# S5 rotation in place, outputs from four products, GLU's first blocks four tiles at a time beside the last S5 blocks

## The chip, the cores and the metric

The kernel runs on one core of one Trainium2 chip. The metric is the device time of one launch in microseconds (us). The kernel before takes 2421.26 us, the median of three runs that lie between 2420.5 and 2422.59 us.

## What is computed

One inference step of a two-layer decoder with 2048 channels, for 256 prompt positions and 8 sample rows (264 columns in all), in float32. Layer 0 is a retention and HGRN2 mixer, layer 1 an S5 state-space layer followed by a GELU-GLU, and each layer ends in a SwiGLU FFN. The change lies in layer 1's mixer, the middle of the program:

```python
def _s5(u, h0_re, h0_im, lam_re, lam_im, log_dt, b_re, b_im, c_re, c_im, d_skip):
    ...
    _, _, hr, hi = lax.associative_scan(_complex_affine_combine, (a_r, a_i, bu_r, bu_i), axis=1)
    y = (jnp.einsum('gcp,blgp->blgc', c_re.astype(jnp.float32), hr)
         - jnp.einsum('gcp,blgp->blgc', c_im.astype(jnp.float32), hi)
         + d_skip.astype(jnp.float32).reshape(S5_GROUPS, S5_GROUP) * ug)
    return y.reshape(B, L, D_MODEL), hr[:, -1], hi[:, -1]

def _odd_mixer(h, s_re, s_im, lam_re, lam_im, log_dt, b_re, b_im, c_re, c_im, d_skip, w_a, w_b):
    y, hr, hi = _s5(h, s_re, s_im, lam_re, lam_im, log_dt, b_re, b_im, c_re, c_im, d_skip)
    z = jax.nn.gelu(y).astype(h.dtype)
    mix = (z @ w_a) * jax.nn.sigmoid(z @ w_b)
    return mix, hr, hi
```

## The kernel before, in words

**The stream of weights.** Every large product is cut into 128x128 weight tiles. A tile is multiplied three times (high part by high part, high by low, low by high: `stream`, L126, L127, L129), which gives float32 accuracy. A unit is up to eight tiles, one 512 KB transfer into a `raw` buffer on SyncE's queue (`load`, L82). `split` makes the high part on ScalarE (`whi`, L88) and the low part by a subtraction (`wlo`, L95) on VectorE, or on GpSimd where `relief` or `every` says so. Each of the three kinds has four buffers; `ahead` runs four splits and eight loads in front of TensorE. `stream` takes segments (block, first tile, last tile) from the list `order`, and after each segment `slot` advances the side work, written as generators that `yield` between their pieces. So the order of the program is written out by hand, and each engine works through its own part in that order.

**S5.** The function `s5` handles the 2048 channels as four blocks `kb` of four channel tiles. The 256 positions are 32 chunks of 8. For each block `products` (TensorE L1316, copied out by ScalarE L1321 into buffers of the `wlo` ring) and `to_states` (transposes, L1329) bring the chunk inputs into PSUM as real and imaginary part, 128x512 each. `turn` (VectorE, L1361 to L1366) rotates them by an angle that grows with the chunk, so that the recurrence has real multipliers; it writes a second pair of PSUM buffers. `scan` runs the two recurrences (L1374) and rotates back in six VectorE operations (L1377 to L1382) into `h`, of which there are two buffers. `inject` (L1339, L1342) puts the direct part of the output into PSUM, and `outputs` (L1392) adds the part from the states: 64 small float32 matmuls (64 rows by 32 columns of weights, 128 moving columns) for each block, with the weights `wcs` that `load_wc` fetches. `activate` (L1406) applies the gelu; `features` (L1412, L1417, L1418) transposes the result into `a2h` and `a2l`, the moving operand of the GLU. `multipliers` (ScalarE L1348, GpSimd L1350) prepares the scan's multipliers `magx`.

**GLU.** `glu` plans 32 output blocks with two units (16 tiles) each. The first four blocks start before all features exist: they run their tiles 0 to 7 block by block, then tiles 8 to 11 of all four, then 12 to 15. `zready` holds the tiles that exist. In the program before, outputs(2) stands ahead of the first GLU matmul, and outputs(3) between GLU segments.

**What sets the order around the change.** SyncE's queue carries the transfers `wb` (L1223), `wc` (L1227) and `w_glu` (L82) in program order. VectorE carries the rotations, the scans, the transposes of the features and most low parts.

Of the kernel before, what the change touches and what calls it, by code (L numbers as in the profile page):

```python
# [46 lines left out]
class Step:  # L47


    def __init__(self, ctx, tc):  # L50
        self.tc, self.nc = tc, tc.nc
        pool = lambda name, **kw: ctx.enter_context(tc.tile_pool(name=name, bufs=1, **kw))
        self.per = pool("per")
        self.wp = pool("wp")
        self.ps = pool("ps", space=bass.MemoryType.PSUM)
        self.dr = pool("dr", space=bass.MemoryType.DRAM)
        ctx.enter_context(tc.manual_schedule())
        self.mx = None
# [1135 lines left out]
def s5(S, I, O, ss, zready):  # L1194
# [98 lines left out]
    Hb = [X[:, 1056 * i:1056 * i + 1056].rearrange("p (r a n) -> p r a n", r=2, a=16) for i in range(2)]  # L1293
# [15 lines left out]
    def products(kb, ks=range(4)):  # L1309

        for k in ks:
# [7 lines left out]
            if k % 2 == 0:  # L1319
                sB[kb, k // 2] = flat(ring("wlo", F32R).bitcast(F32))  # L1320
# [31 lines left out]
    H = {}  # L1352


    def turn(kb, a=0, b=512):
        if a == 0:
            H[kb, "w"] = [S.ps.tile([128, 512], F32, name="acc", bufs=2) if kb < 3 else S.pt() for _ in range(2)]
        c, s = (flat(S.rot[:, i, 16 * kb:16 * kb + 16])[:, a:b] for i in range(2))
        p = [v[:, a:b] for v in pT[kb]]
        w0, w1, t0, t1 = [v[:, a:b] for v in H[kb, "w"]] + [tm[:, i, a:b] for i in range(2)]  # L1360
        V.tensor_mul(w0, p[0], c)  # L1361
        V.tensor_mul(t0, p[1], s)
        V.tensor_mul(w1, p[1], c)
        V.tensor_mul(t1, p[0], s)
        V.tensor_add(w0, w0, t0)
        V.tensor_sub(w1, w1, t1)  # L1366

    def scan(kb):
# [3 lines left out]
        w = H[kb, "w"]  # L1372
        for i in range(2):
            V.tensor_tensor_scan(w[i], flat(mags[kb]), w[i], 0.0, op0=OP.mult, op1=OP.add)  # L1374
        h = H[kb] = Hb[kb % 2]
        f = lambda v: v.rearrange("p (a n) -> p a n", n=32)
        V.tensor_mul(h[:, 0, :, 1:], f(w[0]), f(c))  # L1377
        V.tensor_mul(h[:, 1, :, 1:], f(w[0]), f(s))
        V.tensor_mul(w[0], w[1], s)
        V.tensor_mul(w[1], w[1], c)  # L1380
        V.tensor_sub(h[:, 0, :, 1:], h[:, 0, :, 1:], f(w[0]))
        V.tensor_add(h[:, 1, :, 1:], h[:, 1, :, 1:], f(w[1]))  # L1382
        G.tensor_copy(fin[:, :, 16 * kb:16 * kb + 16], h[:, :, :, 32])
# [25 lines left out]
    def features(kb):  # L1409
        for i in range(2):  # L1410
            zt = new("zt", [128, 512], 2)
            V.transpose(zt, zs[kb, i])  # L1412
            for k in range(2):
# [4 lines left out]
                (G if kb < 3 else V).tensor_sub(v(S.a2l), src, v(S.a2h).bitcast(F32))  # L1418

    def sample():  # L1420
# [6 lines left out]
        t = X[:, 1056:1568]  # L1427
# [5 lines left out]
        G.memset(Hb[1][:, :, :, 0:1], 0.0)  # L1433
# [28 lines left out]
    for kb in range(3):
        scan(kb)
        if kb == 0:
            load_wb(14)
            for kt in range(4, 8):
                load_wc(kt)
        inject(kb)
        if kb == 2:
            features(1)  # L1470
            more()
        multipliers(kb + 1)
        to_states(kb + 1)
        if kb < 2:
            products(kb + 2)
        if kb == 1:
            features(0)
        if kb == 0:
            load_wb(15)
        if kb == 1:  # L1480
            for _ in range(2):
                S.load(S.nd)
                S.nd += 1
        if kb == 2:
            S.relief = 4
            for _ in range(2):
                S.split(S.nsp)
                S.nsp += 1
        outputs(kb)
        activate(kb)  # L1490
    inject(3)
    more()
    for _ in range(2):
        S.split(S.nsp)
        S.nsp += 1
    zready.update(range(8))
# [88 lines left out]
def glu(S, I, zready, after):  # L1585
# [234 lines left out]
```

## Time and profile before

| | us |
|---|---|
| median of three runs | 2421.26 |
| the profiled execution's own time | 2419.22 |
| its span, first to last instruction | 2417.2 |
| TensorE busy in the span | 2368.6 (98%) |
| VectorE busy | 1522.2 (63%) |
| ScalarE busy | 1107.8 (46%) |
| GpSimd busy | 768.0 (32%) |

The span is divided by engine: PE is TensorE's matmuls, PEld its weight loads (they overlap), DVE is VectorE, ACT ScalarE, POOL GpSimd, SP SyncE. Times in the trace count from the span's start; S5's four blocks and GLU's first four blocks lie between about 1390 and 1470 us. A wait of an engine is given with what released it; "issue" means that the engine waited for nothing that the profile shows. A float32 matmul of the program stands as two MATMUL records and two weight loads in the trace.

### The profile page before, as it was taken

The numbers are of one execution on the slowest core, as the hardware profiler recorded it, in microseconds if no ns is written. First come the engines' busy times: TensorE is split into PE (matmuls) and PEld (weight loads), VectorE is DVE, ScalarE is ACT, GpSimd is POOL, SyncE is SP. The second block draws the span as 40 slices with busy tenths as digits, with TensorE's granted clock in tenths as the row PEclk, the third lists the DMA queues.
The fourth block names the chain that finished last, engine by engine and source line by source line (L and its number), as shares of the span: only waits on it lengthen the run. The fifth ranks groups of instructions, "written<-read, shape, count | busy, mean of one in ns | idle before, by whom it ended". The sixth has DMA issues, their size and how long they took to land.

```text
span 2417.2 us, 49487 instructions
## 1 busy us (share of the span) xinstructions
PE 2368.6 (98%) x20331; PEld 2329.5 (96%) x20331; DVE 1522.2 (63%) x2415; ACT 1107.8 (46%) x1612; POOL 768.0 (32%) x739
## 2 busy tenths in 40 slices
PE   8999999999999999999999989999999999999997
PEld 8999999999999999999989969999999999999997
DVE  6777777777888688886755575445444344434444
ACT  6464645554444444444434465444443344434444
POOL 3121121222246565656542352222112211122121
PEclk9999999999999999999999999999999999999999
DMA  7757666765567766677666885556556555565554
GB/s 238 244 202 239 215 225 231 247 198 179 173 208 236 233 227 212 215 230 242 221 192 182 282 329 176 184 184 200 183 184 183 177 183 184 182 183 177 183 167 138
DMA packets 148593, 499.65 MB, mean 207 GB/s; under 512 B 22480, under 2 KB 25024, under 8 KB 147856
## 3 DMA queue, kind: packets, MB, share of 16 engines
q1 hardware_dynamic: 122608, 426.61, 54.7%
q0 software_dynamic: 25760, 69.89, 8.5%
q8 instruction: 160, 2.62, 0.4%
q14 instruction: 65, 0.53, 0.1%
HBM read 452.44 MB, written 43.91 MB: 205 GB/s over the span
## 4 chain that ended last, share of the span: by engine, by line
PE 83%; DVE 9%; ACT 4%; issue 2%; DMA 2%; POOL 0%; DVEq 0%; SPq 0%; ACTq 0%; POOLq 0%
PE acc L126 26%; PE acc L127 25%; PE acc L129 25%; DVE wlo L95 3%; ACT whi L88 2%; PE pa L487 1%; PE pt L1316 0%; DMA raw<-w_in 0%; DVE st L426 0%; DMA whi<-wb 0%; PE pt L1030 0%; PE pt L1015 0%; PE ps L318 0%; PE pt L1668 0%; PE pt L377 0%
## 5 line engine op out<-in xcount | busy, mean ns | idle before, releaser
L126 PE MATMUL acc<-xh,whi 128*128 128x264 f32 x3776 | 1088.4, 288 | 7.3 <-ACT whi L641 7.1
L129 PE MATMUL acc<-xh,wlo 128*128 128x264 f32 x3776 | 1073.7, 284 | 8.3 <-POOL wlo L95 6.0
L127 PE MATMUL acc<-xl,whi 128*128 128x264 f32 x3776 | 1071.2, 284 | 0.0
L88 ACT ACTIVATE whi<-raw 128x1024 fp32r<-128x1024 f32 (+1 forms) x767 | 788.3, 1035 | 399.0 <-PE acc L127 269.2
L95 DVE TENSOR_TENSOR wlo<-raw,whi 128x1024 fp32r<-128x1024 f32 (+1 forms) x591 | 730.7, 1238 | 376.0 <-ACT whi L88 375.9
L95 POOL TENSOR_TENSOR wlo<-raw,whi 128x1024 fp32r<-128x1024 f32 (+1 forms) x176 | 423.7, 2408 | 1231.8 <-ACT whi L88 1209.2
L126 PEld LDWEIGHTS acc<-xh,whi 128*128 128x128 f32 x3776 | 713.5, 189 | 11.3 <-ACT whi L641 7.4
L129 PEld LDWEIGHTS acc<-xh,wlo 128*128 128x128 f32 x3776 | 710.4, 188 | 10.8 <-POOL wlo L95 7.3
L127 PEld LDWEIGHTS acc<-xl,whi 128*128 128x128 f32 x3776 | 714.4, 189 | 0.4
L126 PE MATMUL acc<-a2h,whi 128*128 128x264 f32 x2080 | 594.1, 286 | 0.0
L129 PE MATMUL acc<-a2h,wlo 128*128 128x264 f32 x2080 | 590.2, 284 | 0.6 <-POOL wlo L95 0.4
L127 PE MATMUL acc<-a2l,whi 128*128 128x264 f32 x2080 | 590.2, 284 | 0.1
L126 PEld LDWEIGHTS acc<-a2h,whi 128*128 128x128 f32 x2080 | 392.4, 189 | 1.5 <-issue 1.4
L127 PEld LDWEIGHTS acc<-a2l,whi 128*128 128x128 f32 x2080 | 392.5, 189 | 0.3 <-DVE a2l L1564 0.3
L129 PEld LDWEIGHTS acc<-a2h,wlo 128*128 128x128 f32 x2080 | 390.6, 188 | 1.1 <-POOL wlo L95 0.7
L1563 ACT ACTIVATE a2h<-up 128x264 fp32r<-128x264 f32 x88 | 37.4, 425 | 274.4 <-DVE up L1562 274.4
L170 ACT ACTIVATE sg<-pre 128x264 f32<-128x264 f32 x88 | 37.4, 424 | 219.8 <-DVE pre L1554 219.8
L1569 DVE TENSOR_TENSOR x<-x,acc 128x264 f32<-128x264 f32 x96 | 41.1, 428 | 136.7 <-PE acc L129 136.0
L1554 DVE TENSOR_TENSOR pre<-acc,R 128x264 f32<-128x264 f32 x88 | 37.8, 429 | 123.8 <-PE acc L129 123.7
L1034 POOL DMA_DIRECT2D wb<-kp x128 | 76.7, 608 | 0.0
L1564 DVE TENSOR_TENSOR a2l<-up,a2h 128x264 fp32r<-128x264 f32 x88 | 40.4, 459 | 43.2 <-ACT a2h L1563 43.2
L1561 DVE TENSOR_TENSOR up<-acc,R 128x264 f32<-128x264 f32 x88 | 37.7, 429 | 34.3 <-PE acc L129 34.3
(484 smaller groups left out, 1915.5 us busy)
## 6 DMA issues: line engine op xcount, KB each, us to landing
raw<-w_gu SPq DMA_DIRECT2D x352, 512.0 KB, 3.8
raw<-w_dn SPq DMA_DIRECT2D x128, 512.0 KB, 4.3
raw<-w_in SPq DMA_DIRECT2D x127, 512.0 KB, 4.6
raw<-w_glu SPq DMA_DIRECT2D x64, 512.0 KB, 4.3
raw<-w_dn SPq DMA_DIRECT2D x64, 384.0 KB, 3.6
raw<-w_out SPq DMA_DIRECT2D x32, 512.0 KB, 4.3
st<-sret POOLq DMA_DIRECT2D x16, 512.0 KB, 7.9
o_sret<-st POOLq DMA_DIRECT2D x16, 512.0 KB, 6.4
```

The lines of the kernel that those rows point to most:

```text
L88: self.nc.scalar.activation(u.hi, u.raw, AF.Copy)
L95: e.tensor_sub(u.lo, u.raw, u.hi.bitcast(F32))
L126: mm(k.acc, u.hi[:, j], h, start=k.done == 0, stop=False)
L127: mm(k.acc, u.hi[:, j], l, start=False, stop=False)
L129: mm(k.acc, u.lo[:, j], h, start=False, stop=k.done == k.total)
L170: self.nc.scalar.activation(out, in_, func, **kw)
L1034: G.dma_start(d[16 * j:16 * j + 16, :, 128:].rearrange("c g x -> g c x"), Kp[:, 16 * (7 - j):16 * (7 - j) + 128])
L1554: V.tensor_mul(t, acc, R)
L1561: V.tensor_mul(t, acc, R)
L1563: A.activation(S.a2h[:, k], t, AF.Copy)
L1564: V.tensor_sub(S.a2l[:, k], t, S.a2h[:, k].bitcast(F32))
L1569: V.tensor_add(S.x[:, nt], S.x[:, nt], acc)
```

## The change

- `turn` rotates in place: products with the sine go to SBUF, those with the cosine overwrite the input, and sum and difference are left in the same PSUM buffers. `to_states` takes these buffers in turn from the tags `acc` and `pa`.
- `scan` turns back without additions: it writes four products (four VectorE operations in place of six) into an `h` of four planes, of which there is one buffer in place of two. `outputs` adds the planes on TensorE: 128 matmuls for each block in place of 64. The final states are formed by two additions on GpSimd in place of a copy.
- The copies of products(2) and (3) go to other SBUF space than the `wlo` ring; `wb` 14 and 15 are loaded ahead of `wc` 4 to 7; four loads of `w_glu` come earlier; `relief` is now a set that names which six of the first seven splits run on GpSimd.
- GLU starts ahead of outputs(2): the first four blocks run in segments of four tiles; outputs(2), activate(2), inject(3) and scan(3) come two segments later, features(2) and outputs(3) six segments after that, features(3) last. The low parts of features 2 and 3 are made on VectorE. The first two GLU blocks accumulate in PSUM tag `pt`.

In the changed kernel the numbers of unchanged lines differ by up to 16 (`split` is L94 in place of L95); outputs stays at L1392.

```diff
-        if self.relief > 0:
-            self.relief -= 1
+        if i in self.relief:
             e = self.nc.gpsimd
...
-    Hb = [X[:, 1056 * i:1056 * i + 1056].rearrange("p (r a n) -> p r a n", r=2, a=16) for i in range(2)]
+    h = X[:, :2112].rearrange("p (r a n) -> p r a n", r=4, a=16)
...
-            pT[kb] = [S.pt("a", 2) for _ in range(2)]
+            pT[kb] = [S.ps.tile([128, 512], F32, name=("acc", "pa")[kb % 2], bufs=2) for _ in range(2)]
...
-        w0, w1, t0, t1 = [v[:, a:b] for v in H[kb, "w"]] + [tm[:, i, a:b] for i in range(2)]
-        V.tensor_mul(w0, p[0], c)
-        V.tensor_mul(t0, p[1], s)
-        V.tensor_mul(w1, p[1], c)
-        V.tensor_mul(t1, p[0], s)
-        V.tensor_add(w0, w0, t0)
-        V.tensor_sub(w1, w1, t1)
+        p0, p1, t0, t1 = [v[:, a:b] for v in pT[kb]] + [tm[:, i, a:b] for i in range(2)]
+        V.tensor_mul(t0, p1, s)
+        V.tensor_mul(t1, p0, s)
+        V.tensor_mul(p0, p0, c)
+        V.tensor_mul(p1, p1, c)
+        V.tensor_add(p0, p0, t0)
+        V.tensor_sub(p1, p1, t1)
...
         V.tensor_mul(h[:, 0, :, 1:], f(w[0]), f(c))
-        V.tensor_mul(h[:, 1, :, 1:], f(w[0]), f(s))
-        V.tensor_mul(w[0], w[1], s)
-        V.tensor_mul(w[1], w[1], c)
-        V.tensor_sub(h[:, 0, :, 1:], h[:, 0, :, 1:], f(w[0]))
-        V.tensor_add(h[:, 1, :, 1:], h[:, 1, :, 1:], f(w[1]))
-        G.tensor_copy(fin[:, :, 16 * kb:16 * kb + 16], h[:, :, :, 32])
+        V.scalar_tensor_tensor(h[:, 1, :, 1:], f(w[1]), -1.0, f(s), op0=OP.mult, op1=OP.mult)
+        V.tensor_mul(h[:, 2, :, 1:], f(w[0]), f(s))
+        V.tensor_mul(h[:, 3, :, 1:], f(w[1]), f(c))
+        for i in range(2):
+            G.tensor_add(fin[:, i, 16 * kb:16 * kb + 16], h[:, 2 * i, :, 32], h[:, 2 * i + 1, :, 32])
...
-            for i in range(2):
+            for i in range(4):
...
-                        PE.matmul(pc[kb][r][32 * q:32 * q + 32, 128 * k:128 * k + 128], H[kb][half, i, 4 * k + q, :32],
-                                  W[half, i, q], start=False, stop=i == 1, tile_position=(64 * r, 32 * q),
+                        PE.matmul(pc[kb][r][32 * q:32 * q + 32, 128 * k:128 * k + 128], h[half, i, 4 * k + q, :32],
+                                  W[half, i // 2, q], start=False, stop=i == 3, tile_position=(64 * r, 32 * q),
...
+    scan(2)
+    to_states(3)
+    inject(2)
+    more()
+    split(2)
+    multipliers(3)
+    features(1)
+    more()
+    zready.update(range(4, 8))
+    yield "glu"
+
+    yield
+    outputs(2)
+    activate(2)
     inject(3)
...
     scan(3)
+    for _ in range(5):
+        yield
     features(2)
     zready.update(range(8, 12))
-    yield "glu"
     yield
     outputs(3)
...
-    for b in pairs[1]:
-        b[0].blk.tag = "pa"
-    S.plan([(b[0], 0, 8) for b in first] + [(b[1], 0, 4) for b in first] + [(b[1], 4, 8) for b in first])
+    for b in pairs[0]:
+        b[0].blk.tag = "pt"
+    S.plan([(b[i], j, j + 4) for i in range(2) for j in (0, 4) for b in first])
```

TensorE, from the end of outputs(1): transposes of block 3 follow, and then outputs(2) (`po` and `ps` are its two accumulators). Before:

```order
L1392 MATMUL po<-wcs_16540,xl 32x128
L1392 MATMUL ps<-wcs_16540,xl 32x128
L1329 MATMUL pa<-ident,wlo 128x128 x8
L1392 MATMUL po<-wcs_16533,xl 32x128
L1392 MATMUL ps<-wcs_16533,xl 32x128
```

Now:

```order
L1392 MATMUL po<-wcs_16540,xl 32x128
L1392 MATMUL ps<-wcs_16540,xl 32x128
L1336 MATMUL pa<-ident,xh 128x128 x8
L125 MATMUL pt<-a2h,whi 128x264
L126 MATMUL pt<-a2l,whi 128x264
L128 MATMUL pt<-a2h,wlo 128x264
```

GLU's matmuls (of which 24 come here) stand where outputs(2) stood, and outputs(2) with 128 matmuls comes behind them.

VectorE, the scan of block 1 and what follows it, with the engines that each row waits for (`xl` is the space of `h`). Before:

```order
L1374 SCALAR_TENSOR_TENSOR acc<-magx,acc 128x512 [waits DVE_49,Pool_49]
L1374 SCALAR_TENSOR_TENSOR acc<-magx,acc 128x512 [waits DVE_49]
L1377 TENSOR_TENSOR xl<-acc,rot 128x16x32 [waits DVE_49]
L1378 TENSOR_TENSOR xl<-acc,rot 128x16x32
L1379 TENSOR_TENSOR acc<-acc,rot 128x512 [waits DVE_49]
L1380 TENSOR_TENSOR acc<-acc,rot 128x512
L1381 TENSOR_TENSOR xl<-xl,acc 128x16x32 [waits DVE_49]
L1382 TENSOR_TENSOR xl<-xl,acc 128x16x32 [waits DVE_49]
```

Now:

```order
L1376 SCALAR_TENSOR_TENSOR pa<-magx,pa 128x512 [waits DVE_49,Pool_49]
L1376 SCALAR_TENSOR_TENSOR pa<-magx,pa 128x512 [waits DVE_49]
L1378 TENSOR_TENSOR xl<-pa,rot 128x16x32 [waits DVE_49,PE_49]
L1379 SCALAR_TENSOR_TENSOR xl<-pa,rot 128x16x32 [waits DVE_49,PE_49]
L1380 TENSOR_TENSOR xl<-pa,rot 128x16x32 [waits PE_49]
L1381 TENSOR_TENSOR xl<-pa,rot 128x16x32 [waits PE_49]
```

Two operations are gone, and the four that write `h` now wait for TensorE too: the outputs of the block before read the same buffer.

GpSimd, around the multipliers of block 3 (the MEMSET of `magx`, for which scan(3) waits). Before:

```order
L1350 MEMSET magx 128x16 [waits Activation_49]
L95 TENSOR_TENSOR wlo<-raw,whi 128x1024 [waits DMAHW4_49,PE_49,Activation_49]
L95 TENSOR_TENSOR wlo<-raw,whi 128x1024 [waits DMAHW5_49,PE_49,Activation_49]
L95 TENSOR_TENSOR wlo<-raw,whi 128x1024 [waits DMAHW1_49,PE_49,Activation_49]
L95 TENSOR_TENSOR wlo<-raw,whi 128x1024 [waits DMAHW3_49,PE_49,Activation_49]
L1383 COPY fin<-xl 128x2x16 [waits DVE_49]
```

Now:

```order
L94 TENSOR_TENSOR wlo<-raw,whi 128x1024 [waits DMAHW1_49,Activation_49]
L1383 TENSOR_TENSOR fin<-xl 128x16 [waits DVE_49] x2
L94 TENSOR_TENSOR wlo<-raw,whi 128x1024 [waits DMAHW6_49,Activation_49]
L94 TENSOR_TENSOR wlo<-raw,whi 128x1024 [waits DMAHW7_49,Activation_49]
L1357 MEMSET magx 128x16 [waits Activation_49]
```

The MEMSET has moved behind the splits.

## Rows read from the trace of the kernel before

**Rows 1.** The page, part 1: busy time, share and instructions of each engine.
```profile
PE 2368.6 (98%) x20331; PEld 2329.5 (96%) x20331; DVE 1522.2 (63%) x2415; ACT 1107.8 (46%) x1612; POOL 768.0 (32%) x739
```

**Rows 2.** Windows: busy time of each engine by stretch.
```profile
core 0: us, PE busy (x) PEld busy (x) DVE busy (x) ACT busy (x) POOL busy (x), PEclk, DMA share, GB/s
...
1400.00:1410.00 10.00, 10.00 (x156) 6.68 (x148) 8.95 (x18) 4.81 (x9) 4.51 (x5) 1.00 1.02 399
1410.00:1420.00 10.00, 8.15 (x224) 4.90 (x216) 9.96 (x16) 6.77 (x16) 0.36 (x3) 1.00 1.02 410
1420.00:1430.00 10.00, 5.89 (x152) 3.98 (x152) 9.97 (x16) 5.21 (x13) 3.55 (x6) 0.84 1.03 418
1430.00:1440.00 10.00, 6.75 (x140) 5.77 (x141) 8.12 (x13) 8.07 (x18) 8.22 (x8) 0.67 0.59 226
...
1450.00:1460.00 10.00, 7.02 (x56) 6.60 (x56) 8.34 (x9) 4.16 (x6) 1.44 (x1) 1.00 0.36 113
...
1500.00:1600.00 100.00, 100.00 (x830) 100.00 (x829) 46.78 (x63) 48.23 (x70) 19.90 (x8) 1.00 0.56 183
```

**Rows 3.** Waits of PE, 1390 to 1475: us in total, times, longest.
```profile
PE po L1392 <- issue: 2.6, 1, 2.6
PE pa L126 <- ACT whi L88: 2.2, 1, 2.2
PE ps L1392 <- issue: 2.1, 1, 2.1
...
PE po L1392 <- DMA wcs<-wc: 1.6, 1, 1.6
...
PE pa L129 <- DVE wlo L95: 0.8, 1, 0.8
...
PE acc L129 <- POOL wlo L95: 0.4, 1, 0.4
```

**Rows 4.** Timeline of PE: start, duration, and idle time before it.
```profile
1412.17 0.29 PE L1392 MATMUL po<-wcs,xl 64*32 64x128 f32 x1
...
1422.29 0.29 PE L1392 MATMUL po<-wcs,xl 64*32 64x128 f32 x1
...
1426.34 0.29 PE L1392 MATMUL ps<-wcs,xl 64*32 64x128 f32 x1 [2.10 <-issue]
...
1436.20 0.27 PE L1392 MATMUL po<-wcs,xl 64*32 64x128 f32 x1 [2.60 <-issue]
...
1436.76 0.44 PE L126 MATMUL acc<-a2h,whi 128*128 128x264 f32 x1
...
1467.62 0.28 PE L129 MATMUL pa<-a2h,wlo 128*128 128x264 f32 x1
```

**Rows 5.** Lines of PE, outputs(0), 1412 to 1414.2: busy, mean ns, idle before.
```profile
L1392 PE MATMUL ps<-wcs,xl 64*32 64x128 f32 x64 | 2.0, 271 | 0.0
L1392 PE MATMUL po<-wcs,xl 64*32 64x128 f32 x64 | 2.0, 271 | 0.0
```

**Rows 6.** The page, part 3: queue of instructions over the span (packets, MB, share).
```profile
q8 instruction: 160, 2.62, 0.4%
```

**Rows 7.** The same in 1409–1411, 1416–1417.6, 1423.9–1425.1, 1433.5–1434.8.
```profile
q8 instruction: 1, 0.02, 3.2%
q8 instruction: 1, 0.02, 3.8%
q8 instruction: 1, 0.02, 4.9%
q8 instruction: 1, 0.02, 5.0%
```

**Rows 8.** Lines of DVE and POOL, 1400 to 1470.
```profile
L1382 DVE TENSOR_TENSOR xl<-xl,acc 128x512 f32<-128x512 f32 x3 | 2.0, 679 | 0.0
L1381 DVE TENSOR_TENSOR xl<-xl,acc 128x512 f32<-128x512 f32 x3 | 2.0, 677 | 0.0
...
L95 POOL TENSOR_TENSOR wlo<-raw,whi 128x1024 fp32r<-128x1024 f32 x6 | 14.3, 2401 | 14.0 <-PE acc L129 13.6 <-ACT whi L88 0.5
```

More of the change, by code (lines that the diff above doesn't have):

```diff
@@ L61, in __init__ @@
         self.extra = 0
-        self.relief = 0
+        self.relief = set()
         self.every = 0
@@ L1319, in products @@
             if k % 2 == 0:
-                sB[kb, k // 2] = flat(ring("wlo", F32R).bitcast(F32))
+                if kb < 2:
+                    t = flat(ring("wlo", F32R).bitcast(F32))
+                elif (kb, k) == (2, 0):
+                    t = X[:, 2112:3136]
+                else:
+                    a = 8 * kb + 2 * k - 20
+                    t = U[:, a:a + 4].rearrange("p k r n -> p (k r n)")
+                sB[kb, k // 2] = t
             A.activation(sB[kb, k // 2][:, 512 * (k % 2):512 * (k % 2) + 512], p, AF.Copy)
@@ L1350, in multipliers @@
         G.memset(mags[kb][:, :, 0:1], 0.0)
-    H = {}
     def turn(kb, a=0, b=512):
-        if a == 0:
-            H[kb, "w"] = [S.ps.tile([128, 512], F32, name="acc", bufs=2) if kb < 3 else S.pt() for _ in range(2)]
         c, s = (flat(S.rot[:, i, 16 * kb:16 * kb + 16])[:, a:b] for i in range(2))
-        p = [v[:, a:b] for v in pT[kb]]
-        w0, w1, t0, t1 = [v[:, a:b] for v in H[kb, "w"]] + [tm[:, i, a:b] for i in range(2)]
-        V.tensor_mul(w0, p[0], c)
-        V.tensor_mul(t0, p[1], s)
-        V.tensor_mul(w1, p[1], c)
-        V.tensor_mul(t1, p[0], s)
-        V.tensor_add(w0, w0, t0)
-        V.tensor_sub(w1, w1, t1)
+        p0, p1, t0, t1 = [v[:, a:b] for v in pT[kb]] + [tm[:, i, a:b] for i in range(2)]
[5 more added lines that the diff above has]
+        V.tensor_sub(p1, p1, t1)
     def scan(kb):
@@ L1371, in scan @@
             turn(kb)
[L1372 removed]
+        w = pT[kb]
         for i in range(2):
             V.tensor_tensor_scan(w[i], flat(mags[kb]), w[i], 0.0, op0=OP.mult, op1=OP.add)
[L1375 removed]
         f = lambda v: v.rearrange("p (a n) -> p a n", n=32)
         V.tensor_mul(h[:, 0, :, 1:], f(w[0]), f(c))
[L1378 to L1383 removed]
+        V.scalar_tensor_tensor(h[:, 1, :, 1:], f(w[1]), -1.0, f(s), op0=OP.mult, op1=OP.mult)
[3 more added lines that the diff above has]
+            G.tensor_add(fin[:, i, 16 * kb:16 * kb + 16], h[:, 2 * i, :, 32], h[:, 2 * i + 1, :, 32])
     def outputs(kb):
@@ L1391, in outputs @@
                         half = slice(64 * r, 64 * r + 64)
-                        PE.matmul(pc[kb][r][32 * q:32 * q + 32, 128 * k:128 * k + 128], H[kb][half, i, 4 * k + q, :32],
-                                  W[half, i, q], start=False, stop=i == 1, tile_position=(64 * r, 32 * q),
+                        PE.matmul(pc[kb][r][32 * q:32 * q + 32, 128 * k:128 * k + 128], h[half, i, 4 * k + q, :32],
+                                  W[half, i // 2, q], start=False, stop=i == 3, tile_position=(64 * r, 32 * q),
                                   skip_group_check=True)
             load_wc(4 * kb + k + 8)
-            if kb == 1 and 2 <= k:
-                S.load(S.nd)
-                S.nd += 1
     zs = {}
@@ L1417, in features @@
                 A.activation(v(S.a2h), src, AF.Copy)
-                (G if kb < 3 else V).tensor_sub(v(S.a2l), src, v(S.a2h).bitcast(F32))
+                (G if kb < 2 else V).tensor_sub(v(S.a2l), src, v(S.a2h).bitcast(F32))
     def sample():
@@ L1426, in sample @@
                       tile_position=(0, o), skip_group_check=True)
-        t = X[:, 1056:1568]
+        t = X[:, 2112:2624]
         A.activation(t, p, AF.Copy)
@@ L1458, in s5, with fetch, split @@
     load_wb(13)
-    G.memset(Hb[0][:, :, :, 0:1], 0.0)
+    G.memset(h[:, :, :, 0:1], 0.0)
     products(1)
     more()
[L1462 to L1490, printed above, removed]
-    inject(3)
[L1492 to L1496, printed above, removed]
+    def fetch(n):
+        for _ in range(n):
+            S.load(S.nd)
+            S.nd += 1
+    def split(n):
+        for _ in range(n):
+            S.split(S.nsp)
+            S.nsp += 1
+    S.relief = {S.nsp + i for i in (0, 1, 2, 3, 4, 6)}
+    scan(0)
+    load_wb(14)
+    inject(0)
+    multipliers(1)
+    to_states(1)
+    products(2)
+    load_wb(15)
+    for kt in range(4, 8):
+        load_wc(kt)
+    fetch(2)
+    outputs(0)
+    activate(0)
+    scan(1)
+    inject(1)
+    multipliers(2)
+    to_states(2)
+    products(3)
+    split(1)
+    features(0)
+    split(1)
+    fetch(2)
+    outputs(1)
+    activate(1)
+    zready.update(range(4))
+    scan(2)
[11 more added lines that the diff above has]
+    activate(2)
+    inject(3)
     scan(3)
+    for _ in range(5):
+        yield
     features(2)
     zready.update(range(8, 12))
-    yield "glu"
     yield
```

1 line of the change is left out of this document (removed).

## The prediction

> **What bounds the kernel now.** I read the busy shares first: TensorE is busy for 98% of the span [rows 1], so over the whole program nothing but TensorE work counts, and a change can win only where TensorE waits. The windows show where that is [rows 2]: from 1500 on TensorE is busy 100.00 of 100 us, but in the S5 stretch it is busy 8.15, 5.89 and 6.75 of 10 us (1410 to 1440), and 7.02 in 1450 to 1460. The same rows show two things that run at their limit there: VectorE is busy 8.95, 9.96 and 9.97 of 10 us from 1400 to 1430, and the DMA engines have a share of 1.02 to 1.03. The granted clock falls to 0.84 and 0.67 in 1420 to 1440, behind the two windows in which TensorE waited most.
>
> Then the waits of TensorE [rows 3]. The two largest next to the one on ScalarE (2.2) have no releaser: "issue", 2.6 and 2.1 us, both inside outputs(1) and outputs(2), between two of their matmuls, at 1436.20 and 1426.34 [rows 4]. In both places one packet of the instruction queue q8 moved just before: one in 1433.5 to 1434.8, one in 1423.9 to 1425.1 [rows 7]. So I take these two waits to be TensorE standing without instructions. What supports it: the span has 160 such packets [rows 6] for 20331 matmul and 20331 weight-load records [rows 1], 254 records for each. One outputs block has 128 matmul and as many weight-load records, so it eats one packet in 2.0 us [rows 5]; GLU and FFN need one in about 15 us (1659 records in 100 us) [rows 2]. And while the DMA share is 1.02, packets came in 1409 to 1411, 1416 to 1417.6, 1423.9 to 1425.1 and 1433.5 to 1434.8 [rows 7], some 7, 7.5 and 9.7 us apart from middle to middle.
>
> [...]
>
> **The change part by part, until GLU starts.** Before, the first GLU matmul runs at 1436.76 [rows 4].
>
> *VectorE.* Two operations of 0.68 us [rows 8] go from each block, 1.36 us; `turn` keeps its six. VectorE has no idle time from 1410 to 1430 [rows 2], so the chain is 2.7 us earlier behind two blocks: outputs(1) could start at 1422.29 [rows 4] less 2.7, about 1420. That the new operations write with a wait for TensorE costs nothing while outputs of the block before has ended; if it has not, the scan waits for it, and everything behind it on VectorE.
>
> *TensorE.* outputs doubles: 256 matmul records by 2.0 us for 128 [rows 5], 3.8 us counting start to start. outputs(1) then ends at about 1424; the eight transposes of block 3 follow (about 1 us, an estimate from 271 ns for one small matmul [rows 5]), and GLU's first matmul waits for the last sample features and its own split, on ScalarE behind the eight operations of activate and inject. I put that at 1429, between 1425, where nothing would be late, and 1432. outputs(2) with its waits (1.6 for `wcs`, 2.6 for instructions) [rows 3] no longer stands ahead. Without any new stall GLU so begins 7.5 us earlier.
>
> *Instructions.* outputs(0) and (1) now want a packet each more, in the stretch where they come 7 us apart. outputs(0) starts at 1412.17 [rows 4], now some 1.3 earlier; it is half done 1.9 us later, at about 1413, and wants the packet which before moved in 1416 to 1417.6 [rows 7]. From the start of the window in which a packet moved to the matmul that resumed it was 2.4 and 2.7 us [rows 4, 7], so this one lets TensorE go on at about 1418.5: a stall of **5.5 us**. The bounds are 0 (packet hidden) and 7.8 (packets 9.7 us apart, less the 1.9 of work). I take 5.5, by the packets nearest in time. VectorE's four writes of block 1 wait for this outputs, as the order shows, so the stall goes into the chain. outputs(1) comes some 9 us later, and its own extra packet is late by less: 1.5 (0 to 3). Small waits at packet ends, 0.3. Together 7.3, so GLU starts at 1436.76 - 7.5 + 7.3: **-0.2 us** (-7.5 to +2.9).
>
> **From GLU's start to the end of its first four blocks** (1436.76 to 1467.62, 192 matmuls by three [rows 4]). Before, only outputs(3) lies in it, 2.0 us [rows 5]; now outputs(2) and (3) at 3.8 each: **+5.6 us**, on TensorE, which is the path here. Each brings one extra packet. The DMA share is 0.59 and less by then [rows 2], so they are late by less: 1.4 and 2.0, **+3.4 us** (0 to 5; the nearest rows, 2.1 and 2.6, are from the saturated stretch). The other waits were 2.2, 0.8 and 0.4 [rows 3], 3.4 in all. Now the features of 2 and 3 come later against GLU's segments, four units are wanted within the first four segments, and the next block's high part is not ready at the end (about 1.8): 3.2 to 3.6, so **-0.2 us** at the lower end, +2 at worst.
>
> *Steps that I cost at nothing.* The MEMSET of `magx` behind two splits on GpSimd of 2.4 us [rows 8] holds scan(3) for about 2 us; outputs(3) comes six segments later (72 matmuls by 0.12, as 830 in 100 us [rows 2], 8.7 us), which covers it; without that cover it would cost its 2 us. The loads have the same bytes in another order, and the two `wb` ahead of `wc` serve products(3), not late before. The final states' additions on GpSimd (two small ones) have no reader until the end. [...]
>
> **Sum:** -0.2 + 5.6 + 3.4 - 0.2 = **+8.6 us**. It is made against the profiled execution (2419.22, span 2417.2), which lies 2.0 below the median of the runs; on the median it gives 2421.3 + 8.6, **2430 us**. About 0.2% (4.8 us) is what a measurement of this kernel can tell from no change.
>
> **The rivals.**
>
> *Packets stay hidden.* If the doubled outputs finds its instructions there, the terms 7.3 and 3.4 go: -7.5 + 5.6 - 0.2 = -2.1, of which I give 0.8 back, because GLU then starts within the stretch of low clock (0.67 [rows 2]) and reaches the features of block 3 sooner than they exist. -1.3: **2420 us**, no change. For it: outputs(0) before had no wait at all [rows 5]. Against it: rows 3. [...]
>
> *The waits vanish: faster.* GLU's matmuls fill the places where TensorE stood. The idle time is 4.1 and 3.3 us in 1420 to 1440 and 3.0 in 1450 to 1460 [rows 2], 10.4 in all; the added TensorE work in that stretch is 5.6. If all of it is filled, -4.8, and with VectorE's saving, as far as it brings the last features forward, -5 to -6: **2416 us**. For it: VectorE and TensorE are both off their limit behind 1440. Against it: outputs(0) and (1) stand ahead of all GLU work, and a stall there moves the start of the filling. It decides if the first GLU matmul runs by 1430 and TensorE waits under 2 us between there and the end of the four blocks.
>
> *Packets come later still.* If the stretch of full DMA lasts longer (the `w_glu` loads are moved into it), 9.7 us between packets is the rate for all of them: 7.8 at outputs(0), 3 at outputs(1), and 2 to 3 at each of the last two, some 5.5 more than the sum: **2435 us**. For it: the last distance in rows 7 is the longest. Against it: it contains a wait for `wcs`.
>
> **How the numbers follow.** The forecast (+5 to +11) has 0.46; packets later still 0.16; packets hidden 0.23; waits vanish 0.15. Slower by over 0.2%: the first two, less a share of the forecast whose end lies under +4.8, 0.61. Within 0.2%: packets hidden and that share, 0.24. Faster: the third, 0.15. The likeliest case's own range is 2426 to 2432; since the others are of both signs, the range that holds 8 in 10 reaches to the packets-later case above (2437) and down to 2417, which leaves out most of the faster case.
>
> **What would show it.** In the profile after: outputs(0) with an "issue" wait of about 5 us in its middle and a q8 packet just before it ends; VectorE's writes of `h` in block 1 waiting for TensorE by about as much; the first GLU matmul near 1436.5; an "issue" wait of 1 to 2.5 us in outputs(2) and (3) each; the 576th GLU matmul record near 1476. I am wrong if "issue" waits are absent though outputs has 256 records of matmuls, or if GLU starts before 1431, or if the time is lost behind the first four GLU blocks, where the program has not changed.

## The result, and the profile after

The changed kernel takes **2436.7 us** (median of four runs, 2436.22 to 2437.09), the kernel before 2420.88 (four runs beside it): ratio 1.0066, 95% interval 1.0048 to 1.0083, 15.8 us slower. The forecast was 2430 us, 2417 to 2437, slower with a chance of 0.61. The side and the mechanism came out; the size is nearly twice that of the forecast, at the end of the range. Runs of one kernel spread by a few us (the kernel before lies between 2416.85 and 2424.3 in all its runs here), so a term of a few tenths, read from one profile of each kernel, is a reading of that execution.

The page of the changed kernel, parts 1 and 3, shows the added work (before: [rows 1, 6]):

```profile
PE 2380.9 (98%) x20843; PEld 2340.9 (96%) x20843; DVE 1521.1 (62%) x2410; ACT 1108.5 (46%) x1612; POOL 768.2 (32%) x739
...
q8 instruction: 164, 2.69, 0.4%
```

There are 512 matmul records and 512 weight loads more, and four more instruction packets. TensorE is busy for 12.3 us more; the span is 17.6 us longer. The waits of TensorE in the changed kernel, 1385 to 1500 (us in total, times, longest), answer to [rows 3]:

```profile
PE po L1392 <- issue: 7.2, 2, 5.0
PE ps L1392 <- issue: 3.6, 2, 2.8
PE acc L125 <- ACT pre L1608: 2.4, 1, 2.4
PE pt L125 <- ACT a2h L1438: 1.4, 1, 1.4
...
PE pt L128 <- issue: 1.1, 1, 1.1
```

The waits for `wcs`, for `wb` and for the split are gone. In their place there are 10.9 us of waits without a releaser inside outputs, where there were 4.7. The timeline of TensorE shows where they are (start, duration, idle time before), beside [rows 4]:

```profile
1397.20 0.42 PE L1316 MATMUL pt<-xl,xh 128*32 128x256 f32 x4 [0.73 <-issue]
...
1413.93 0.29 PE L1392 MATMUL po<-wcs,xl 64*32 64x128 f32 x1
...
1421.84 0.37 PE L1392 MATMUL po<-wcs,xl 64*32 64x128 f32 x1 [5.00 <-issue]
...
1432.63 0.29 PE L1392 MATMUL ps<-wcs,xl 64*32 64x128 f32 x1 [0.86 <-issue]
...
1437.47 0.42 PE L1392 MATMUL ps<-wcs,xl 64*32 64x128 f32 x1 [2.79 <-issue]
...
1441.48 0.59 PE L125 MATMUL pt<-a2h,whi 128*128 128x264 f32 x1 [1.45 <-ACT a2h L1438]
...
1452.72 0.27 PE L1392 MATMUL po<-wcs,xl 64*32 64x128 f32 x1 [2.24 <-issue]
...
1483.00 0.28 PE L128 MATMUL acc<-a2h,wlo 128*128 128x264 f32 x1
1485.68 0.39 PE L125 MATMUL acc<-a2h,whi 128*128 128x264 f32 x1 [2.40 <-ACT pre L1608]
```

The places of these waits say what TensorE waits for. Between the two waits inside outputs(1), at 1432.63 and 1437.47, it works through 128 MATMUL records and 128 weight loads (L1392 alone: busy time and records of PE and PEld, granted clock, DMA share, GB/s):

```profile
1432.60:1437.00 4.40, 2.06 (x128) 1.79 (x128) 1.00 0.98 367
```

That is one packet, 254 records on average [rows 1, 6]. And in the ten profiles of this study every one of the 35 issue waits in outputs and GLU's first four blocks ends 2.2 to 2.7 us after the start of a packet (the wait of 5.00: 2.27 us after the packet of 1419.57).

S5's first matmul (L1316) starts at 1397.20; before, this row reads

```profile
1395.67 0.42 PE L1316 MATMUL pt<-xl,xh 128*32 128x256 f32 x4 [0.73 <-issue]
```

The code ahead of it is unchanged, and in the ten profiles it starts between 1393.9 and 1398.2, so I count from it: 1.5 us of the difference of the two profiles lie ahead of the change. From there the first GLU matmul stands at 44.3 us (before 41.1, from 1436.76 [rows 4]), the last of the first four blocks at 85.8 (before 71.9, from 1467.62), and the 401st GLU matmul, well inside the unchanged part, at 113.7 (before 97.7). The loss of 16.0 us is thus 3.2 before GLU starts, 10.7 inside its first four blocks, and 2.2 behind them (the wait of 2.40 for an accumulator).

The prediction's text has a slip in a count: the first four blocks are 192 matmuls in all (64 tiles by three), not 192 by three, and the matmul that it puts near 1476 is the 192nd. No term rests on it.

The windows of the changed kernel answer to [rows 2], with the same columns:

```profile
1410.00:1420.00 10.00, 6.84 (x259) 4.53 (x258) 6.39 (x9) 2.39 (x4) 0.31 (x2) 1.00 0.95 354
1420.00:1430.00 10.00, 8.16 (x151) 5.16 (x158) 7.38 (x13) 5.00 (x13) 0.61 (x3) 0.66 0.98 395
1430.00:1440.00 10.00, 6.35 (x264) 5.06 (x249) 5.78 (x8) 6.12 (x13) 8.40 (x8) 0.85 0.89 298
1440.00:1450.00 10.00, 8.55 (x227) 8.18 (x233) 7.13 (x11) 5.80 (x12) 7.54 (x7) 0.64 0.70 251
1450.00:1460.00 10.00, 7.76 (x114) 7.29 (x97) 2.58 (x4) 3.01 (x9) 1.01 (x3) 0.83 0.01 5
...
1470.00:1480.00 10.00, 9.03 (x60) 8.87 (x61) 5.28 (x7) 4.97 (x10) 1.98 (x1) 0.83 0.34 114
```

VectorE, which was at its limit (9.96 of 10 us), is now busy 6.39 and 7.38: the bound has gone from VectorE to TensorE's waits. The granted clock is 0.64, 0.83 and 0.83 in the last three of these windows, where the kernel before had 0.98 from 1440 to 1450 and 1.00 behind that:

```profile
1440.00:1450.00 10.00, 10.00 (x193) 9.66 (x193) 5.43 (x10) 6.48 (x12) 9.42 (x9) 0.98 0.55 181
```

That VectorE waits for TensorE is in its own waits (1395 to 1480): the writes of `h`, of which there is one buffer, wait for the outputs of the block before. The second line is scan(3), held by the MEMSET of `magx`.

```profile
DVE xl L1378 <- PE ps L1392: 9.1, 3, 6.2
...
DVE pa L1376 <- POOL magx L1357: 1.9, 1, 1.9
```

### The profile page after: what moved, and what is told of

Its sections match the earlier page's. It is cut to its first block, busy times and chain, and to the rows that moved or that the text cites. A ratio compares the mean times of both kernels' runs of the same rounds, so it can differ in the third digit from the quotient of the medians.

```text
span 2434.8 us, 50506 instructions
## 1 busy us (share of the span) xinstructions
PE 2380.9 (98%) x20843; PEld 2340.9 (96%) x20843; DVE 1521.1 (62%) x2410; ACT 1108.5 (46%) x1612; POOL 768.2 (32%) x739
## 4 chain that ended last, share of the span: by engine, by line
PE 82%; DVE 9%; ACT 3%; issue 3%; DMA 1%; POOL 1%; SPq 0%; DVEq 0%; ACTq 0%; POOLq 0%
PE acc L125 25%; PE acc L126 25%; PE acc L128 25%; DVE wlo L94 3%; ACT whi L88 2%; PE pa L486 1%; PE pt L1316 1%; DVE st L425 0%; PE pt L1029 0%; PE po L1392 0%; PE ps L317 0%; DVE T L1079 0%; DMA raw<-w_in 0%; PE pt L1014 0%; DVE up L1578 0%
## 5 line engine op out<-in xcount | busy, mean ns | idle before, releaser
L94 DVE TENSOR_TENSOR wlo<-raw,whi 128x1024 fp32r<-128x1024 f32 (+1 forms) x590 | 732.7, 1243 | 383.0 <-ACT whi L88 382.8
L94 POOL TENSOR_TENSOR wlo<-raw,whi 128x1024 fp32r<-128x1024 f32 (+1 forms) x177 | 427.1, 2413 | 1246.7 <-ACT whi L88 1237.5
L1585 DVE TENSOR_TENSOR x<-x,acc 128x264 f32<-128x264 f32 x96 | 41.1, 428 | 136.0 <-PE acc L128 135.2
```

The source lines that it names most:

```text
L1585: V.tensor_add(S.x[:, nt], S.x[:, nt], acc)
```

## The experiments

Theory 1: the doubled outputs runs ahead of the supply of instruction packets. Theory 2: the loss comes from the new order or from the single `h`. Theory 3, next to 1: the supply has one rate, whatever the DMA engines do. half_width, products_old_order, sums_on_dve and less_dma ran beside 15 runs of the kernel before (median 2421.8), the others beside 22 (median 2421.35).

### half_width: the old kernel with twice the instructions

```diff
-                        PE.matmul(pc[kb][r][32 * q:32 * q + 32, 128 * k:128 * k + 128], H[kb][half, i, 4 * k + q, :32],
-                                  W[half, i, q], start=False, stop=i == 1, tile_position=(64 * r, 32 * q),
-                                  skip_group_check=True)
+                        for c in (0, 64):
+                            PE.matmul(pc[kb][r][32 * q:32 * q + 32, 128 * k + c:128 * k + c + 64], H[kb][half, i, 4 * k + q, :32],
+                                      W[half, i, q, c:c + 64], start=False, stop=i == 1, tile_position=(64 * r, 32 * q),
+                                      skip_group_check=True)
```

> The kernel before, with one edit: each outputs matmul is cut into two of half the moving width (64 columns in place of 128), so that outputs issues 128 matmuls for a block over the same columns and sums; nothing else moves. If TensorE stands for want of instructions (theory 1), outputs(0) shows an issue wait of 4 to 5 us in its middle, outputs(1) and (2) waits of 1 to 4 us, and the time is 5 to 9 us over the kernel before (2426 to 2430). If the loss of the changed kernel comes from its order, its single h or its added sums (theory 2), this kernel has no new wait and is within 2 us of the kernel before.

Measured: 2429.2 us, ratio 1.0036 (1.0022 to 1.005), 7.4 us slower. Waits of TensorE, 1392 to 1510:

```profile
PE po L1393 <- issue: 7.5, 2, 4.0
PE ps L1393 <- issue: 6.7, 4, 2.2
```

The wait of 4.0 is in outputs(0), where there was none before; outputs(1) has 1.3 and 2.2, outputs(2) 2.2 and 1.0, outputs(3) 3.5. Order, `h`, rotations and loads are those of the kernel before, so the number of instructions alone makes these waits; neither the new order nor the single `h` is needed for them. The expectation said that the kernel works over the same columns; its records do not cost half, though. In the lines of TensorE, 1410.3 to 1413.1, before the wait,

```profile
L1393 PE MATMUL ps<-wcs,xl 64*32 64x64 f32 x96 | 2.7, 221 | 0.0
L1393 PE MATMUL po<-wcs,xl 64*32 64x64 f32 x96 | 2.6, 221 | 0.0
```

192 records take 2.7 us, 14 ns each, where 128 records of twice the width took 2.0 [rows 5], 16 ns each. So each block also takes some 1.6 us more of TensorE's time (256 by 14 ns less 2.0 us) beside the waits; how the 7.4 us divide between the two was not measured.

### products_old_order: the new rotation and outputs in the old order

```diff
+    h = X[:, :2112].rearrange("p (r a n) -> p r a n", r=4, a=16)
...
+        V.scalar_tensor_tensor(h[:, 1, :, 1:], f(w[1]), -1.0, f(s), op0=OP.mult, op1=OP.mult)
+        V.tensor_mul(h[:, 2, :, 1:], f(w[0]), f(s))
+        V.tensor_mul(h[:, 3, :, 1:], f(w[1]), f(c))
...
-            for i in range(2):
+            for i in range(4):
...
```

> The kernel before with the new turn, scan and outputs (rotation in place, four products in one h, 128 matmuls for a block) but the old order: outputs(2) ahead of GLU, old plan of the GLU segments, old loads. Theory 1: waits of 4 to 5 us in outputs(0) and 1 to 3 us in each later outputs; 5 to 10 us over the kernel before. Theory 2 in the form that the new order costs the time: no more than 2 us over the kernel before, or faster, as VectorE saves 1.3 us for each block.

Measured: 2431.58 us, ratio 1.0038 (1.0026 to 1.0051), 9.8 us slower. Waits of TensorE, 1392 to 1510:

```profile
PE po L1384 <- issue: 7.4, 3, 3.9
PE ps L1384 <- issue: 6.4, 3, 3.1
```

3.9 in outputs(0), and 3.3, 3.4 and 3.1 in the others: theory 1, with a little less in outputs(0) and a little more behind it than expected. The waits also stand at the same records. In the changed kernel, in half_width and here TensorE stops behind the 192nd MATMUL record of outputs(0) and behind the 118th and the 246th of outputs(1); in the kernel before and in sums_on_dve, where outputs has half the records, behind the 118th of outputs(1). The times and the order differ between these kernels, so the place of a wait follows the count of instructions. What VectorE saves is not to be seen in the time: it waits for outputs. Against half_width the four products cost 2.4 us more, though they take two operations a block from VectorE; the two intervals overlap. So the single `h`, the rotation in place and the saved operations together cost little, if anything, in the old order.

### sums_on_dve: the new order without the doubling

```diff
         V.tensor_mul(h[:, 3, :, 1:], f(w[1]), f(c))
         for i in range(2):
-            G.tensor_add(fin[:, i, 16 * kb:16 * kb + 16], h[:, 2 * i, :, 32], h[:, 2 * i + 1, :, 32])
+            V.tensor_add(h[:, 2 * i, :, 1:], h[:, 2 * i, :, 1:], h[:, 2 * i + 1, :, 1:])
...
-            for i in range(4):
+            for i in range(2):
...
-                        PE.matmul(pc[kb][r][32 * q:32 * q + 32, 128 * k:128 * k + 128], h[half, i, 4 * k + q, :32],
+                        PE.matmul(pc[kb][r][32 * q:32 * q + 32, 128 * k:128 * k + 128], h[half, 2 * i, 4 * k + q, :32],
...
```

> The changed kernel, with VectorE adding the planes of h in pairs again (two more operations for each block) and 64 outputs matmuls for each block; the new order of S5 and GLU and the single h stay. Theory 1: the wait in outputs(0) goes, the first GLU matmul comes at 1431 to 1434 us, and the time is within 3 us of the kernel before (2418 to 2424). Theory 2, that the order or the single h costs the time: it stays at 2432 or more.

Measured: 2424.5 us, ratio 1.0011 (1.0002 to 1.002), 2.7 us slower than the kernel before (as expected, though 0.5 above the range in us), 12.2 faster than the changed kernel; each against the kernel before beside it, the difference is 13.1. The first GLU matmul is at 1432.81, and outputs(0) has no wait. So in the new order the doubling costs 12 to 13 us, and the rest of the change (order, single `h`, rotation in place) about 3. The waits, 1392 to 1510, say where the 3 may be:

```profile
PE pt L125 <- ACT a2h L1440: 4.2, 1, 4.2
PE ps L1394 <- issue: 2.5, 1, 2.5
PE acc L125 <- ACT pre L1610: 2.4, 1, 2.4
```

Two of these were not there before: GLU's first matmul waits 4.2 us for the operand of the sample rows, and the fifth block waits 2.4 us for an accumulator, since the four interleaved blocks now end together, the two in `acc` last, and the next blocks want `acc` again. The one of 2.5 is the old wait of outputs(1), behind the same record.

### less_dma and light_dma: the same instructions with fewer bytes

less_dma:

```diff
-            SY.dma_start(wcs[kt % 8], S.wc[kt].rearrange("p i q x -> p (i q x)"))
+            w = 1024 if kt < 4 else 128
+            SY.dma_start(wcs[kt % 8][:, :w], S.wc[kt].rearrange("p i q x -> p (i q x)")[:, :w])
```

> The changed kernel, with the output weights wc of channel tiles 4 to 15 loaded to an eighth of their columns only (so the outputs of those tiles are computed from stale weights): the DMA share falls below 1 from about 1415 on. If packets of instructions are late because the DMA engines are full (theory 1), the wait in outputs(0) falls from 5.0 to 2 to 3.5 us, those in outputs(1) from 3.6 in all to 1 or less, and the time to 2428 to 2433. If TensorE cannot fetch more than one packet in some 5 us whatever the DMA engines do (theory 3), the waits stay as they are, within 0.5 us.

Measured: 2433.85 us, ratio 1.0051 (1.0038 to 1.0063). The wait in outputs(0) is 4.2, in outputs(1) one of 2.7, in outputs(2) one of 2.6: the first two are above the expectation of theory 1, below that of theory 3. The edit had missed its place: the DMA share was still 0.92 from 1410 to 1420, and 0.21 only behind that. light_dma takes four further transfers of 512 KB away, ahead of outputs(0):

```diff
         for h in hs:
+            if kt >= 14:
+                WB[kt, h] = WB[kt - 2, h]
+                continue
```

> The kernel less_dma, and wb of channel tiles 14 and 15 are not loaded either (their products use the weights of tiles 12 and 13): from about 1408 on the DMA engines are no longer full, so that outputs(0) is reached too. If the full DMA engines set the wait in outputs(0), it falls from 5.0 (4.2 in less_dma) to 1.5 to 2.5 us, the spacing of the packets from 7 to 3.5 to 4.5 us, and GLU starts 4 to 7 us earlier than in less_dma. If the supply has one rate whatever the DMA engines do, the wait stays over 3.5 us.

Measured: 2429.19 us, ratio 1.0029 (1.0018 to 1.0041). The timeline of light_dma:

```profile
1418.18 0.27 PE L1396 MATMUL po<-wcs,xl 64*32 64x128 f32 x1 [1.39 <-issue]
```

The wait in outputs(0) falls from 5.0 to 1.4 us. Windows of the changed kernel between the starts of two packets (there the queue q8 has one packet in 1411.6 to 1412.0 and one in 1419.4 to 1419.8):

```profile
1411.80:1419.60 7.80, 5.04 (x232) 3.57 (x225) 4.59 (x6) 2.01 (x4) 0.00 (x0) 1.00 0.93 338
```

and of light_dma, between its packets (one each in 1410.6 to 1411.0, 1415.4 to 1415.8 and 1419.1 to 1419.6):

```profile
1410.80:1415.60 4.80, 4.80 (x180) 3.15 (x177) 4.80 (x8) 2.39 (x4) 0.10 (x2) 1.00 0.76 282
1415.60:1419.30 3.70, 2.31 (x151) 1.84 (x135) 1.31 (x2) 0.00 (x0) 0.00 (x0) 1.00 0.19 51
```

The same instructions come 4.8 and 3.7 us apart in place of 7.8, with DMA shares of 0.76 and 0.19 in place of 0.93. So the full DMA engines make most of the wait in outputs(0), and theory 3 falls. But 3.7 us at a share of 0.19 is still more than outputs needs for one packet, 256 records in 2.0 us [rows 5]: a rest stays (1.4 in outputs(0), 0.8 and 1.4 in outputs(1), 2.2 in outputs(2)). In the changed kernel itself the wait of 2.24 in outputs(2) passes while the DMA engines are nearly idle (share 0.02):

```profile
1450.40:1452.80 2.40, 0.16 (x10) 0.08 (x15) 0.69 (x1) 0.00 (x0) 0.13 (x1) 1.00 0.02 7
```

So lighter loads shorten the waits but do not remove them. Both kernels leave weights out, and with them waits for `wb` and `wc`, so how much of the time that they gain over the changed kernel (7.5 us in light_dma) is the supply alone is not shown.

### late_half: one doubled outputs where the DMA engines are not full

```diff
+                        n = 64 if kb == 3 else 128
+                        for c in range(0, 128, n):
```

> The kernel before, with the outputs matmuls of block 3 alone cut into two halves of 64 columns (128 matmuls there, 64 in the other blocks). outputs(3) lies between GLU matmuls, where the DMA share is 0.3 to 0.55. If 512 matmul and load records in a run always outrun the supply, whatever the DMA engines do, outputs(3) shows an issue wait of 1.8 to 3.5 us and the time is 2 to 4 us over the kernel before. If packets are only late where the DMA engines are full, no wait and a time within 1 us of the kernel before.

Measured: 2422.03 us, ratio 1.0004 (0.9995 to 1.0013), no difference. All waits of TensorE, 1446 to 1500:

```profile
PE po L1394 <- issue: 2.1, 1, 2.1
PE acc L129 <- DVE wlo L95: 0.3, 1, 0.3
```

The wait came as expected, 2.1 us, at a DMA share of 0.46 (1449.1 to 1452.5), and the time did not. Before, two waits for a split stood a few us behind (2.2 and 0.8 [rows 3]); they are gone. So a wait for instructions in outputs(3) of the old order is paid out of waits that follow it anyway, and the loss of half_width and products_old_order lies in the earlier blocks: their first GLU matmul stands at 49.3 and 51.7 us behind S5's first matmul, where it was 41.1.

### tags_swapped and dve_sums_mended: what the new order can be brought to

tags_swapped is the changed kernel with

```diff
-    for b in pairs[0]:
+    for b in pairs[1]:
         b[0].blk.tag = "pt"
```

> The changed kernel, with the PSUM tags of GLU's first four blocks exchanged (first pair acc, second pair pt). In the changed kernel the 193rd GLU matmul waits 2.4 us for the accumulator that the fourth block leaves last. If that wait is worth its length on the path, it goes and the time falls by 2 to 2.7 us, to 2434 to 2435. If another wait takes its place (the split of the next unit), under 1 us is gained.

Measured: 2433.3 us, ratio 1.0049 (1.0036 to 1.0063), where the changed kernel has 1.0066 (1.0048 to 1.0083). The wait for the accumulator is gone from the profile. The medians lie 3.4 us apart, more than the wait's 2.4; the intervals overlap, so the gain has the expected sign and about its size, no more can be said. In the profiles the 401st GLU matmul comes 2.4 us earlier (111.3 in place of 113.7), the length of the wait.

dve_sums_mended is sums_on_dve with the same exchange, and

```diff
     products(3)
+    more()
     split(1)
     features(0)
+    more()
     split(1)
...
     inject(2)
-    more()
+    multipliers(3)
     split(2)
-    multipliers(3)
     features(1)
-    more()
```

> The kernel sums_on_dve with three small moves: tags exchanged as in tags_swapped, the MEMSET of the multipliers ahead of two splits on GpSimd, and the gelu and operands of the sample rows made ahead of outputs(1) in place of behind inject(2). If the new order loses only by these waits (2.4 for the accumulator, 4.2 for the sample rows' operand, up to 2 for the MEMSET), it comes to 2417 to 2421, at or below the kernel before. If the order itself costs the time (half clock at an earlier GLU start, features of blocks 2 and 3 that come no sooner), it stays at 2422 to 2424.

Measured: **2419.6 us**, ratio to the kernel before 0.999 (0.9981 to 0.9999): well below the changed kernel, and 1.75 us, 0.1%, below the kernel before, at the edge of what these runs can tell from no change. It is the first case of the expectation: with these waits mended, no loss by the order is left to measure. The first GLU matmul is at 1430.72:

```profile
1430.72 0.56 PE L125 MATMUL acc<-a2h,whi 128*128 128x264 f32 x1 [1.68 <-DVE xl L1380]
```

That is 33.9 us after S5's first matmul (1396.82) in place of 41.1, and yet the time is hardly shorter, as the next section says.

## Why the prediction was right, and where its size was off

**Instructions, outputs(0): right.** Forecast 5.5 us, measured 5.00; without the doubling 0.0; half_width, with the old order, 4.0. The bound from the nearest packets (7 us apart) held: the two packets around it start 7.8 us apart. VectorE's writes of `h` waited for it (6.2 us), as the order had shown. That the size came so near is in part luck: TensorE stopped three quarters through the block, not halfway, and the packet came later, so that, counted from S5's first matmul, the wait began 2.3 us later than forecast and ended 1.8 later.

**VectorE's saving: wrong place.** The step said that outputs(0) starts 1.3 us earlier, since VectorE has no idle time. It starts at 16.7 us behind S5's first matmul, where it was 16.5: TensorE is busy 10.00 of 10 us from 1400 to 1410 [rows 2], and outputs(0) stands behind its products. From there on VectorE waits for TensorE (6.39 of 10 us busy), and the saving has nothing to act on.

**Instructions, outputs(1): the old wait left out.** Forecast for its extra packet 1.5; measured are 0.86 + 2.79 = 3.65, against the one wait of 2.10 that stood there before [rows 4], 1.55 more. So the extra was right in size. But the step let outputs(1) end at about 1424, 3.8 us behind its start and without the wait that it already had, and these 2.1 us are missing from the sum.

**GLU's start: +3.2 in place of -0.2.** The saving that did not come (1.5) and the old wait (2.1) are about the size of this error; smaller ones of both signs cancel, such as the work of outputs(0), 4.45 us beside its wait in place of 3.8 (its last quarter ran at a granted clock of 0.50). The term of -7.5 was too favourable by itself: without the doubling (sums_on_dve) GLU started 36.8 us behind S5's first matmul, only 4.3 earlier than before. Two slips of the prediction belong here: from 1436.76 to 1429 are 7.8 us, not 7.5, and the step's upper bound is 3.6 by its own terms (-7.5 + 7.8 + 3 + 0.3), not 2.9.

**Inside the first four blocks: +10.7, forecast +8.8.** outputs(2) and (3) with their waits take 10.3 us, the time between the GLU matmuls on either side of them (less one normal step), against 2.05 for outputs(3) before: +8.3, where 5.6 + 3.4 had been forecast: a wait of 2.24 in outputs(2), none in outputs(3), and one of 1.1 among the GLU matmuls behind it. The other gaps between GLU matmuls, that one among them, came to 2.1 us after 4.2: -2.1. What is missing in the forecast is the **clock**: the sum has no term for it, so GLU's steps stand in it as before, an estimate of mine that no run had shown. (The prediction puts the low clock of 1420 to 1440 behind the windows in which TensorE waited most; by [rows 2] these are the same windows.) Counted between neighbouring GLU matmuls, 58 steps of the first 192 run at about 0.22 us in place of 0.12, where 14 did before: 5.9 us lost against 1.4, +4.5. Of the 58, 51 start where the granted clock is 0.50, and 10 of the 14 before. The sum is 8.3 - 2.1 + 4.5 = 10.7. The windows above show the same. Of the steps costed at nothing, the MEMSET held scan(3) for 1.9 us, about as forecast, and outputs(3) started without a wait.

**Behind the four blocks: +2.2, a wrong cause.** I had put 1.8 us there for the next unit's split, inside a sum of small waits. The wait is 2.40 for the accumulator, and the exchange of tags removes it. Time lost behind the first four blocks was one of the prediction's signs of being wrong; it came true for these 2.2 us, not for the rest.

**The rivals.** "Packets stay hidden" is excluded by the 10.9 us of waits in outputs, 5.0 us of them at one packet. "Packets come later still" gave 2435 with 9.7 us between packets; the time came out so, but for other reasons (clock, accumulator): the packets were 7.8, 6, 4.7 and 4.8 us apart. That 2436.7 lies inside the range is therefore luck: this rival set the upper end, and the likeliest case's own range ended at 2432. "The waits vanish" needed the first GLU matmul by 1430; it came at 1441.48. dve_sums_mended meets that nearly and gains 1.75 us, not 5. Its windows are

```profile
1430.00:1440.00 10.00, 8.77 (x152) 8.14 (x152) 10.00 (x13) 6.21 (x12) 10.00 (x9) 0.54 1.01 406
1440.00:1450.00 10.00, 10.00 (x154) 9.78 (x150) 8.50 (x10) 4.76 (x10) 6.82 (x8) 1.00 0.35 115
1450.00:1460.00 10.00, 8.43 (x125) 7.08 (x111) 5.62 (x9) 6.31 (x12) 2.39 (x1) 1.00 0.47 151
1460.00:1470.00 10.00, 8.82 (x54) 8.04 (x53) 4.61 (x8) 5.32 (x10) 2.40 (x1) 0.83 0.23 75
```

GLU starts earlier into the lower clock (0.54 from 1430 to 1440), and TensorE waits again in 1450 to 1470 (8.43 and 8.82 of 10 us), for features that come one tile at a time. Counted from S5's first matmul, its GLU starts 7.2 us earlier than in the kernel before, and its first four blocks take 7.8 us longer: 3.2 are outputs(2), which only moved from ahead of GLU into it, 3.4 the steps of 0.22 us (47 against 14), 1.3 other gaps. In the profiles the steps of 0.22 us are 44 to 60 of 192 in sums_on_dve, dve_sums_mended, tags_swapped and the changed kernel, 38 and 27 in light_dma and less_dma, but 4 to 18 in the kernels of the old order, however many instructions outputs has. That is a count of GLU's steps, not of the low clock itself. Between 1380 and 1520 us the stretches at a granted clock of 0.50 add up to 10.2 us in the kernel before and 23.9 in the changed kernel,

```profile
1426.71:1433.54 6.83, 5.25 (x121) 4.43 (x117) 5.24 (x10) 4.87 (x14) 2.02 (x4) 0.50 1.02 419
1436.95:1440.37 3.42, 3.03 (x13) 2.72 (x13) 3.42 (x5) 3.36 (x9) 3.14 (x2) 0.50 0.42 127
...
1419.93:1426.76 6.83, 4.92 (x84) 3.67 (x87) 4.14 (x7) 2.82 (x9) 0.48 (x2) 0.50 1.02 412
1436.99:1447.23 10.24, 8.31 (x42) 7.19 (x43) 6.56 (x11) 7.58 (x17) 7.77 (x8) 0.50 0.71 244
1454.06:1457.47 3.41, 3.41 (x17) 3.41 (x17) 1.06 (x2) 2.21 (x7) 0.43 (x2) 0.50 0.02 5
1471.13:1474.54 3.41, 3.41 (x17) 3.41 (x18) 2.22 (x3) 1.24 (x3) 0.85 (x1) 0.50 0.46 149
```

and to 17.1 in half_width and in products_old_order, 20.5 in sums_on_dve and 10.2 in light_dma. So the low clock grows with the doubling in the old order too; there most of it lies on S5's matmuls and on waits, while in the new order more of it lies on GLU's. In the changed kernel each of the four falls came inside a wait for instructions or at most 1.4 us behind one. Whether the order or these waits make the clock fall was not tried by itself.

**The chain of causes, then.** The change takes two VectorE operations from each block and gives TensorE 64 matmuls more. Those are 256 instructions more for a block, in a stretch where packets came 6.6 to 9.7 us apart before and come 4.7 to 7.8 us apart now. outputs waits for packets; through the single `h` VectorE waits for outputs; GLU starts 3 us later in place of 7 earlier; in the new order it then runs longer at the lower clock (23.9 us at 0.50, before 10.2), and its four blocks end together on the accumulators that the next two want. Of 15.8 us 12 to 13 go with the doubling in the new order (sums_on_dve) and about 3 with the rest. In the old order the doubling, with the single `h` and the rotation, costs 9.8 (products_old_order); 9.8 and 2.7 are 3 us short of 15.8, which the intervals allow, so whether the two make each other worse stays open. A second buffer for `h` was not tried: with four planes there was no space for it in `xl` beside the copies of the products.

## What to carry to other kernels

Where a change trades a few VectorE operations for many small matmuls, count TensorE's instructions, not its columns: a run of some 500 records within 4 us outran the packets in every place tried here but outputs(3) of the new order (waits of 0.8 to 5.0 us), most where loads fill the DMA engines (in outputs(0) 5.0 us at a DMA share of 0.93, 1.4 at 0.76). An "issue" wait of TensorE with a packet on the instruction queue 2.2 to 2.7 us before its end is that wait here, and the two small ones in the profile before the change were a warning: with twice the instructions in the old order, the waits of 2.10 and 2.60 us in outputs(1) and (2) became 3.3 and 3.4 in all (products_old_order). A wait that is there already belongs in the sum beside the one that is added. And when blocks are interleaved so that they end together, look at which accumulator the next block wants, and at the clock of the stretch in which they start.

## What the runs showed of the hardware

- The records (matmuls and weight loads) between the starts of two packets were 457 in the changed kernel with its wait of 5.0 us (232 + 225 in the window above) and 467 in half_width with 4.0; in the kernel before, where the two packets around outputs(0) were 6.6 us apart and TensorE did not wait, they were 408:

```profile
1409.90:1416.50 6.60, 6.60 (x208) 4.38 (x200) 6.60 (x10) 4.37 (x11) 0.30 (x2) 1.00 1.02 409
```

  In the changed kernel they were 540 (271 + 269) around outputs(3), where TensorE did not wait either:

```profile
1463.20:1468.56 5.36, 5.36 (x271) 5.03 (x269) 3.85 (x6) 2.28 (x5) 0.00 (x0) 1.00 0.57 193
```

  So TensorE had more records at hand in these places than one packet's 254, in the last one about twice as many. How much it holds at most was not measured by itself.
- The shortest distance of two packets in the ten profiles was 3.3 us, in less_dma at a DMA share of 0.04:

```profile
1446.61:1449.92 3.31, 1.07 (x39) 1.07 (x43) 0.61 (x2) 0.00 (x0) 0.48 (x1) 0.76 0.04 14
```

  Even that is about 254 records in 3.3 us, 13 ns for each, while outputs without a wait uses 256 in 2.0 us [rows 5], 8 ns for each.
- A float32 matmul record of 64 rows by 32 columns took 14 ns of TensorE's busy time with 64 moving columns (half_width) and 16 ns with 128 [rows 5]; from start to start, over the first 40 records of outputs(0), 13.6 and 14.3 ns. Halving the width saved next to nothing.
